# One plain block in place of two at the start of the last three channel mixers, with the next block's weights finished ahead

## The chip, the cores and the metric

The kernel runs on one core of one Trainium2 chip. The metric is the device time of one execution in microseconds (us), the median of the runs; less is better.

## The reference

A decoder trunk of two layers over 512 tokens of width 1024, all in float32. Each layer is channel mixer, token mixer, channel mixer; the token mixer of the first layer is latent attention, that of the second is sparse attention. So there are four channel mixers, numbered `idx` 0 to 3 here. Cut to what matters:

```python
D_MODEL, SEQ, DEPTH, FFN_HIDDEN = 1024, 512, 2, 2816

def swiglu(x, w_gate, w_up, w_down):
    return (jax.nn.silu(x @ w_gate) * (x @ w_up)) @ w_down

for i in range(DEPTH):
    h = h + 0.5 * swiglu(rmsnorm(h, ffn_norm_a[i]), ffn_a_w_gate[i], ffn_a_w_up[i], ffn_a_w_down[i])
    h = h + mixer_i(rmsnorm(h, mix_norm[i]))
    h = h + 0.5 * swiglu(rmsnorm(h, ffn_norm_b[i]), ffn_b_w_gate[i], ffn_b_w_up[i], ffn_b_w_down[i])
return rmsnorm(h, final_norm)
```

## The kernel before

The activations stand transposed: eight tiles `h[c]` of 128 features by 512 tokens. Every float32 operand of a matmul is split into a high part (a copy rounded by ScalarE) and a low part (the rest, subtracted by VectorE), and a product is three matmuls: high by high, high by low, low by high (`split`, L173; L177 and L178). So each weight costs a DMA, a ScalarE copy and a VectorE subtraction before TensorE can use it.

A channel mixer (`ffn`, from L416) goes through the 22 blocks of 128 hidden units, `f` = 0 to 21. A block computes gate and up for 128 hidden units and 512 tokens, then Silu(gate) x up in parts (`gate`, `act`, `parts`). It comes in two forms:

- **Plain** (`plain`, L404): gate, then up, each 8 chunks of input features times 2 halves of the tokens times 3 matmuls of 256 columns.
- **Seven products** (`product`, L371): gate and up together are a 2 by 2 problem (weights: gate and up, each with two halves of the input features; inputs: two halves of the features, each with two halves of the tokens). A scheme of the Strassen kind does it in 7 products of 4 chunks times 3 matmuls of 256 columns. It needs sums of weights (`wsums`, L328: products 1 and 2 take the gate's weights as they are, 7 and 4, 6 and 3, and 5 take sums) and sums of inputs (`combine`, L231: once per mixer, four calls with `p` = 0 to 3, each giving a quarter of what products 4 to 7 read).

`PLAIN = 3, 2, 2, 2` (L50) says how many blocks at the start of each mixer are plain. While they run, ScalarE and VectorE make the sums of inputs, and the norm's row (1/rms per token) is made: four small matmuls and more (`norm_col`), a transposition, and a round trip through DRAM on POOL's queue (`norm_row`, L293 and L295). The plain blocks don't need the row; their gate does (`plain_acts`, L428 to L430, L439).

The weights of the plain blocks of mixers 1 to 3 are split ahead of time. From block `READY` = 12 of the mixer before, each block loads one eighth (256 KB, `make_load`, L388, on SP's queue) and splits the one that it loaded a block earlier into two spare quarters of the input tiles; POOL's queue writes them to DRAM (`make`, L396). `made_slab` (L401) later reads high and low of a whole slab of 1 MB in one DMA. All other blocks load gate and up raw (`rg`, L333; `ru` or `wr`, L339; 512 KB each) and make sums and splits on the spot.

What sets the order: a scheduler lays down one fixed order for each engine and each DMA queue from the order of the program and estimates of when things are ready; every queue then works in that order. Buffers come from pools with tags: `fh` and `fl` (three each) hold the sums of inputs while they are made (`y`, `u`) and the split weights of products 7, 4, 6, 3; the tiles `w0` to `w2` hold plain slabs and the weights of products 1 and 2; `fr` (three) and `wr` (two) hold raw weights. In PSUM the tags are `mm` (2 banks), `S` (2), `T` (3), `o` (1). A block of seven products uses one bank of each of the first three: `x` (S), `q` (mm), `g` (T). The products go in the order 1, 7, 6, 2, 5, 4, 3, with ScalarE copying intermediate results out of the banks between them (L533, L535, L537, L540). From block 3 on, units of the down projection (`unit`, L169 to L171 on TensorE, L464, L458) are mixed into the blocks.

## Time and profile before

| | us |
|---|---|
| median of 3 runs | 1856.08 |
| lowest, highest run | 1854.83, 1859.17 |
| the profiled execution | 1855.04 |
| its span in the profile | 1853.3 |
| start of the plain blocks of mixers 1, 2, 3 in the span | 543.2, 877.7, 1507.2 |

The profile is one execution. A row of a timeline has the start in us from the span's beginning, the duration, the engine (PE is TensorE, PEld its weight loads, DVE is VectorE, ACT is ScalarE, POOL is GpSimd, SP the queue that issues most DMAs), the line of the kernel, the operation, the tile written and those read, and in brackets how long the engine sat idle before it and what ended that. A row of grouped instructions has the count, the busy time in us, the mean in ns, and the idle time before them. A row of windows has the stretch, its length, then busy time (and count) for PE, PEld, DVE, ACT and POOL, then the granted clock of TensorE, the busy share of the DMA engines, and GB/s. A row of waits has who waited for whom, the sum in us, how often, and the longest. A row of DMA issues has what is written and read, the queue, the count, the size of each, and the median time from issue to landing.

### The profile page before, as it was taken

To read this page: it belongs to the slowest core of one execution; us is meant where nothing else is said; L and a number is where in the kernel's file an instruction comes from. 1 tells how busy PE (TensorE), PEld (TensorE's weight loads), DVE (VectorE), ACT (ScalarE), POOL (GpSimd) and SP (SyncE) were. 2 spreads that over 40 slices of the span, in tenths; PEclk is the share of its full clock that TensorE was granted. 3 is DMA by queue.
4 is the path that set the end of the run, shared out by engine and by line. 5 is a ranking of instruction groups with operands and counts; after the bars stand their busy time and mean duration, and the time that the engine had idled before them with its cause. 6 is when DMAs were issued, how large, how long until landed. Compare 5 with 4: busy or idle time off the path is not lost.

```text
span 1853.3 us, 32953 instructions
## 1 busy us (share of the span) xinstructions
PE 1834.6 (99%) x12392; PEld 1674.9 (90%) x12392; DVE 1529.1 (83%) x2785; ACT 1090.8 (59%) x2033; POOL 275.9 (15%) x398
## 2 busy tenths in 40 slices
PE   8999999999999999999999999999999999999998
PEld 8999999888889999998999999988888889999997
DVE  7988886578779888876998888755988979888885
ACT  7555554579766555544655555426977856555554
POOL 0000000156510000000000000015665500000000
PEclk9999999999999999999999999999999999999999
DMA  7334433142352345433333443233222143333321
GB/s 259 118 120 154 154 124 105 56 110 72 95 176 99 105 143 166 160 115 122 110 115 130 161 160 99 91 106 108 75 86 74 47 163 121 108 107 103 103 90 57
DMA packets 88047, 216.31 MB, mean 117 GB/s; under 512 B 11176, under 2 KB 39232, under 8 KB 87888
## 3 DMA queue, kind: packets, MB, share of 16 engines
q1 hardware_dynamic: 80272, 195.01, 33.2%
q0 software_dynamic: 4512, 14.17, 2.0%
q10 hardware_dynamic: 3104, 5.03, 0.8%
q8 instruction: 97, 1.59, 0.4%
q14 instruction: 62, 0.51, 0.1%
HBM read 192.33 MB, written 14.76 MB: 112 GB/s over the span
## 4 chain that ended last, share of the span: by engine, by line
PE 87%; DVE 7%; ACT 2%; issue 1%; DMA 1%; POOL 1%; SPq 0%; DVEq 0%; ACTq 0%; POOLq 0%
PE pd L169 8%; PE pd L171 8%; PE pd L170 8%; PE px L376 5%; PE px L377 5%; PE px L378 5%; PE pg L376 4%; PE pg L378 4%; PE pg L377 4%; PE pq L376 4%; PE pq L377 4%; PE pq L378 4%; PE o L1295 2%; PE pt L1270 2%; PE po L169 2%; PE po L171 2%
## 5 line engine op out<-in xcount | busy, mean ns | idle before, releaser
L170 PE MATMUL pd<-al,wd 128*128 128x512 f32 x576 | 224.1, 389 | 0.0
L171 PE MATMUL pd<-ah,wd 128*128 128x512 f32 x576 | 224.0, 389 | 0.0
L169 PE MATMUL pd<-ah,wd 128*128 128x512 f32 x576 | 224.0, 389 | 0.0
L376 PE MATMUL px<-four,wh 128*128 128x256 f32 x632 | 175.3, 277 | 2.8 <-ACT uq L537 1.4
L178 DVE TENSOR_TENSOR w<-rg,w 128x1024 fp32r<-128x1024 f32 x79 | 96.3, 1222 | 96.4 <-ACT w L177 96.4
L376 PE MATMUL pq<-four,wh 128*128 128x256 f32 x632 | 174.5, 276 | 0.4 <-DVE tu L439 0.4
L378 PE MATMUL px<-four,wl 128*128 128x256 f32 x632 | 174.7, 276 | 0.0
L377 PE MATMUL px<-four,wh 128*128 128x256 f32 x632 | 174.5, 276 | 0.0
L377 PE MATMUL pq<-four,wh 128*128 128x256 f32 x632 | 174.5, 276 | 0.0
L378 PE MATMUL pq<-four,wl 128*128 128x256 f32 x632 | 174.5, 276 | 0.0
L458 DVE SCALAR_TENSOR_TENSOR h<-pd,h 128x512 f32<-128x512 f32 x216 | 147.0, 681 | 6.1 <-PE pd L171 6.1
L177 ACT ACTIVATE wd<-wdr 128x384 fp32r<-128x384 f32 x192 | 98.5, 515 | 67.9 <-PE pd L170 38.3
L171 PEld LDWEIGHTS pd<-ah,wd 128*128 128x128 f32 x576 | 108.2, 188 | 22.5
L169 PEld LDWEIGHTS pd<-ah,wd 128*128 128x128 f32 x576 | 108.1, 188 | 19.3
L170 PEld LDWEIGHTS pd<-al,wd 128*128 128x128 f32 x576 | 108.1, 188 | 19.4
L376 PEld LDWEIGHTS px<-four,wh 128*128 128x128 f32 x632 | 118.6, 188 | 4.1 <-ACT uq L537 2.1
L177 ACT ACTIVATE w<-rg 128x1024 fp32r<-128x1024 f32 x79 | 83.8, 1060 | 61.9 <-PE pg L378 56.6
L376 PEld LDWEIGHTS pq<-four,wh 128*128 128x128 f32 x632 | 118.6, 188 | 0.5 <-ACT w L177 0.5
L378 PEld LDWEIGHTS px<-four,wl 128*128 128x128 f32 x632 | 118.6, 188 | 0.4 <-DVE wl L178 0.2
L396 POOL DMA_DIRECT2D made<-x x48 | 26.0, 542 | 622.9 <-ACT pg L533 404.5
L377 PEld LDWEIGHTS px<-four,wh 128*128 128x128 f32 x632 | 118.6, 188 | 0.0
L378 PEld LDWEIGHTS pq<-four,wl 128*128 128x128 f32 x632 | 118.6, 188 | 0.0
(368 smaller groups left out, 6059.6 us busy)
## 6 DMA issues: line engine op xcount, KB each, us to landing
wr<-in_w_gu SPq DMA_DIRECT2D x81, 512.0 KB, 4.1
rg<-in_w_gu SPq DMA_DIRECT2D x79, 512.0 KB, 3.4
wdr<-in_w_down SPq DMA_DIRECT2D x192, 192.0 KB, 2.4
made<-x POOLq DMA_DIRECT2D x48, 256.0 KB, 2.8
w<-made SPq DMA_DIRECT2D x12, 1024.0 KB, 5.3
wm<-in_w_gu SPq DMA_DIRECT2D x24, 256.0 KB, 3.9
wdr<-in_w_down SPq DMA_DIRECT2D x24, 256.0 KB, 2.7
wr<-in_mla_w_o SPq DMA_DIRECT2D x8, 512.0 KB, 3.6
```

The source lines that it names most:

```text
L169: mm(out, wh, xh, start=first, stop=False)
L170: mm(out, wh, xl, start=False, stop=False)
L171: return mm(out, wl, xh, start=False, stop=last)
L177: nc.scalar.activation(hi, src, AF.Copy)
L178: (nc.gpsimd if pool else nc.vector).tensor_tensor(lo, src, f32v(hi), op=ALU.subtract)
L376: mm(out, wh[:, p], xh, start=first and p == 0, stop=False, skip_group_check=True)
L377: mm(out, wh[:, p], xl, start=False, stop=False, skip_group_check=True)
L378: mm(out, wl[:, p], xh, start=False, stop=last and p == KP - 1, skip_group_check=True)
L396: self.nc.gpsimd.dma_start(d[:, z, i % 2, :], f32v(t))
L458: nc.vector.scalar_tensor_tensor(self.h[c], p, 0.5, self.h[c], op0=ALU.mult, op1=ALU.add)
L1270: nc.tensor.transpose(pt[:, j * P : j * P + P], p_sb[:, j * P : j * P + P], self.ident)
L1295: mm(out, vs[g][:, j, br * P : (br + 1) * P], x, start=False, stop=last and t == 1 and j == 2 * z + 1, skip_group_check=True)
```

## The change

Mixers 1 to 3 start with one plain block and not two; block `f` = 1 becomes a block of seven products. All four `combine` calls follow the one plain block. The finished weights of that block, sums included, are made in the mixer before, as the plain slabs' were: `PLACES` says at which block `f` each piece is begun. For one plain block these are four eighths of plain slabs (blocks 9 to 11, each split a block later) and two halves of the sums (begun at blocks 12 and 16, four steps over four blocks each: load, then three with splits and 256-wide adds). What block 1 needs is read back as one slab of 1 MB (`g`: products 1 and 2, into a `w` tile), two pairs of 512 KB (`u`: 7 and 4; `h`: 6 and 3; into `fh` and `fl`) and one pair of 256 KB (`s`: 5). In that block alone the products are ordered 1, three quarters of 7, half of 2, the last quarter of 7, 6, the rest of 2, 5, 4, 3. `wsums` for `f` = 2 is now the one held behind the ScalarE copies of the block before it.

```diff
-PLAIN = 3, 2, 2, 2
+PLAIN = 3, 1, 1, 1
-READY = 12
+PLACES = {2: [...],
+          1: [(9, 0, 0, 0), (9, 0, 0, 1), (10, 0, 1, 0), (11, 0, 1, 1), (12, 1, 0, 0), (16, 1, 0, 1)]}
...
         nc, fp, w_gu = self.nc, self.fp, self.a["w_gu"]
+        if (idx, f, "g") in self.made:
+            return self.made_sums(idx, f)
...
-    def product(self, j, w, out, first, last):
+    def product(self, j, w, out, first, last, ps=range(KP)):
...
+    def make_sums(self, idx, f, x, tp):
...
+        def load():
+            for z in range(2):
+                got.append(self.make_load(self.a["w_gu"][idx, f, z].rearrange("p (e x c) -> p e x c", e=2, x=2)[:, :, x]))
...
+        def first():
+            self.make_split(got[0], 0, to("g"))
+            got.append(tp.tile([P, S], F32, tag="sq", bufs=1, name="sm")[:, :HS])
+            u = got[1]
+            nc.vector.tensor_tensor(got[2], u[:, :HS], u[:, HS:], op=ALU.add)
+            nc.vector.tensor_tensor(u[:, :HS], u[:, :HS], got[0][:, :HS], op=ALU.add)
+
+        def second():
+            self.make_split(got[1], 1, to("u"))
+            g = got[0]
+            nc.vector.tensor_tensor(g[:, :HS], g[:, :HS], got[2], op=ALU.add)
+            nc.vector.tensor_tensor(g[:, HS:], g[:, HS:], g[:, :HS], op=ALU.add)
+
+        def third():
+            self.make_split(got[0], 0, to("h"))
+            self.make_split(got[2], 1, self.made_tile(idx, f, "s").rearrange("p (z x c) -> p z x c", z=4, x=2)[:, :2, x])
...
+    def made_sums(self, idx, f):
...
+        use(1, 2, *self.made_slab(idx, f, "g"))
+        for name, i, j in (("u", 7, 4), ("h", 6, 3)):
+            hl = self.sum_tiles(1024)
+            for z in range(2):
+                nc.sync.dma_start(f32v(hl[z]), self.made[idx, f, name][:, z * 1024 : z * 1024 + 1024])
+            use(i, j, *hl)
+        hi = fp.tile([P, S], F32R, tag="sh", bufs=2, name="wh")
+        lo = fp.tile([P, S + 2 * PAD], F32R, tag="sl", bufs=2, name="wl")[:, 2 * PAD :]
+        for z, t in enumerate((hi, lo)):
+            nc.sync.dma_start(f32v(t), self.made[idx, f, "s"][:, z * S : z * S + S])
+        use(5, None, hi, lo)
+        return w
...
-            for p in (((0, 1), (2, 3)) if plain == 2 else ((0, 1), (2,), (3,)))[f]:
+            for p in {1: ((0, 1, 2, 3),), 2: ((0, 1), (2, 3)), 3: ((0, 1), (2,), (3,))}[plain][f]:
                 self.combine(p)
...
-            self.product(7, w, q, True, False)
+            self.product(7, w, q, True, False, range(KP - (f == 1)))
+            if f == 1:
+                self.product(2, w, g[:, :HS], False, False, range(2))
+                self.product(7, w, q, False, False, range(KP - 1, KP))
...
-            self.product(2, w, g[:, :HS], False, True)
+            self.product(2, w, g[:, :HS], False, True, range(2 * (f == 1), KP))
...
-            if idx + 1 < len(PLAIN):
-                i = f - READY
-                if 0 < i <= 4 * PLAIN[idx + 1]:
-                    self.make(idx + 1, i - 1)
-                if 0 <= i < 4 * PLAIN[idx + 1]:
-                    self.make_load(idx + 1, i)
+            for step in make.get(f, []):
+                step()
```

## The prediction

> **What bounds the kernel now.** I read the page first, then the windows around the second mixer's start, then TensorE's waits, then the timelines of each engine there.

> ```profile
> span 1853.3 us, 32953 instructions
> PE 1834.6 (99%) x12392; PEld 1674.9 (90%) x12392; DVE 1529.1 (83%) x2785; ACT 1090.8 (59%) x2033; POOL 275.9 (15%) x398
> L376 PE MATMUL px<-four,wh 128*128 128x256 f32 x632 | 175.3, 277 | 2.8 <-ACT uq L537 1.4
> ```
> ```profile
> 543.22:565.94 22.72, 22.72 (x202) 22.72 (x200) 21.07 (x34) 15.37 (x20) 2.30 (x3) 1.00 0.54 198
> 565.94:575.46 9.52, 9.52 (x87) 9.52 (x85) 9.37 (x13) 8.32 (x14) 0.00 (x0) 1.00 0.25 85
> 575.46:586.46 11.00, 9.96 (x86) 9.71 (x85) 11.00 (x19) 5.84 (x12) 0.00 (x0) 1.00 0.26 88
> ```

> TensorE is the bound nearly everywhere, so fewer matmuls should mean less time; the question is how much one costs. The first window holds the two plain blocks (192 matmuls and the 8 small ones of the norm), the second the first block of seven products (84 matmuls), the third the second such block. 9.52 / 84 = 0.113 us for a 256-column matmul. The 277 ns of its row is its stay in the pipeline, which overlaps its neighbours'. [...]

> VectorE (third busy column) is full through all three windows: the start of a mixer is where TensorE has company. Its waits there:

> ```profile
> PE px L376 <- ACT uq L537: 1.4, 2, 0.7
> PE px L376 <- ACT pg L533: 1.3, 2, 1.0
> 579.38 0.39 PE L376 MATMUL px<-four,wh 128*128 128x256 f32 x1 [1.04 <-ACT pg L533]
> 1545.92 0.39 PE L376 MATMUL px<-four,wh 128*128 128x256 f32 x1 [0.69 <-ACT uq L537]
> ```

> Each of the three mixers loses 1.04, 0.7 and 0.69 us in its second block of seven products, 2.4 us in all, with some 0.1 us for the restart (the matmul after a wait takes 0.39 us in place of 0.277).

> **Matmuls removed.** A plain block has 2 x 8 x 2 x 3 = 96 matmuls, a block of seven products 7 x 4 x 3 = 84. Each mixer swaps one: 12 x 0.113 = 1.36 us, three mixers 4.08 us. All of it is on TensorE's own path, where nothing covers it.

> **Combines, now due earlier.** Product 7 needs the sums of inputs at block f = 1, after one plain block and not two. In the second mixer the plain block would end at 543.22 + 96 x 0.113 + 0.95 (the norm's matmuls, what the first window leaves over 192 x 0.113) = 555.05. VectorE's rows of the four combines:

> ```profile
> 546.17 0.68 DVE L244 TENSOR_TENSOR u<-y 128x512 f32<-128x512 f32 x1
> 549.77 0.41 DVE L246 TENSOR_TENSOR u<-y,u 128x256 f32<-128x256 f32 x1
> 551.34 1.18 DVE L178 TENSOR_TENSOR four<-u,four 128x1024 fp32r<-128x1024 f32 x1
> 552.78 1.22 DVE L178 TENSOR_TENSOR four<-u,four 128x1024 fp32r<-128x1024 f32 x1
> ...
> 555.46 1.23 DVE L178 TENSOR_TENSOR four<-u,four 128x1024 fp32r<-128x1024 f32 x1
> ...
> 560.14 1.22 DVE L178 TENSOR_TENSOR four<-u,four 128x1024 fp32r<-128x1024 f32 x1
> ```

> The fourth ends at 561.4, behind four instructions on weights of the first block, which the change takes from there: two adds and two 1024-wide splits, 3.5 us by their starts (0.6, 0.6, 1.14, 1.14; each overlaps the next by 0.08). Without them it ends near 557.8, if ScalarE's halves keep up. Its user, the last quarter of product 7, stands behind product 1 (12 matmuls), three quarters of 7 (9) and half of 2 (6): 555.05 + 27 x 0.113 = 558.1. It just fits; I take 0. Without the new order product 7 would need it at 557.4, a wait of 0.4 us a mixer: that is what the order is worth.

> **Weights of block f = 1 from DRAM.** 7 and 4, then 6 and 3, come into tiles `fh`/`fl`, three buffers each, which the combines hold. I assume that buffers are handed out in program order: then the low half of 7 waits for the second combine's `u`, read last by L178 (552.78 + 1.22 = 554.0; the high half only for its `y`, free after L246 at 550.2), and the low half of 6 for the third's (about 556.7). No transfer of this kind is in the trace; the nearest are:

> ```profile
> rg<-in_w_gu SPq DMA_DIRECT2D x2, 512.0 KB, 3.1
> rg<-in_w_gu SPq DMA_DIRECT2D x1, 512.0 KB, 6.4
> 547.00:549.00 2.00, 2.00 (x21) 2.00 (x19) 2.00 (x5) 2.00 (x4) 0.00 (x0) 1.00 1.02 416
> 553.00:555.00 2.00, 2.00 (x20) 2.00 (x19) 2.00 (x4) 0.64 (x1) 0.00 (x0) 1.00 0.89 358
> 555.00:557.00 2.00, 2.00 (x20) 2.00 (x20) 2.00 (x4) 1.80 (x3) 0.10 (x1) 1.00 0.04 14
> ```

> 512 KB land in 3.1 us on a quiet queue (issues after 551) and 6.4 us behind others (issue at 543.98). At 554.0 the plain slabs and the slab for 1 and 2 should be in (the change has one slab less to bring before then than the kernel now), so I take 3.1: landing 557.15. Product 7 wants it at its third matmul, 555.05 + 14 x 0.113 = 556.6. Wait 0.5 us, with restart 0.65, times three: +1.95. Ends: 0 (the buffer is free sooner, or TensorE has other products ahead of it) and 3.95 a mixer (6.4 us). The low half of 6 lands by 559.9 and is wanted near 560.0: 0, at worst another 0.5. SP issues in order, so a transfer that waits for `fl` also holds back what stands behind it, the `rg`/`wr` of later blocks; they are due a block later, and I put that at 0.

> **VectorE's load at the start.** Rows for the sum:

> ```profile
> L178 DVE TENSOR_TENSOR w<-rg,w 128x1024 fp32r<-128x1024 f32 x79 | 96.3, 1222 | 96.4 <-ACT w L177 96.4
> L178 DVE TENSOR_TENSOR wl<-s,wh 128x512 fp32r<-128x512 f32 x79 | 53.9, 683 | 3.0 <-ACT wh L177 3.0
> L364 DVE TENSOR_TENSOR rg<-rg 128x512 f32<-128x512 f32 x79 | 54.5, 690 | 2.1
> L542 DVE TENSOR_TENSOR tu<-px,uq 128x256 f32<-128x256 f32 x79 | 32.9, 417 | 10.4 <-ACT pg L540 10.4
> ...
> 569.31 2.35 DVE L178 TENSOR_TENSOR w<-rg,w 128x1024 fp32r<-128x1024 f32 x2
> 574.04 1.22 DVE L178 TENSOR_TENSOR w<-rg,w 128x1024 fp32r<-128x1024 f32 x1
> ```

> One block's weights cost 3 x 1.22 + 0.68 + 4 x 0.69 = 7.1 us. Up to the third block f = 3 VectorE makes those of f = 2 and f = 3 before and after alike, since f = 1 got its weights from DRAM either way; the new block adds two adds of 0.42 us. So at f = 3 VectorE is 0.83 us later by work and TensorE 1.36 - 0.65 = 0.7 us earlier: up to 1.5 us more wait there. Against it: the weights of f = 2 no longer have to stand between the combines, and of the three splits of `rg` at 569.31 and 574.04 only one can be for f = 3, so VectorE worked 2.4 us ahead before that wait: its order has slack. Ends per mixer -0.9 (the wait goes) and +1.5; I take 0, the present wait staying.

> **The gate.** TensorE's `pu` bank of the plain block is wanted by product 7 of f = 2 at about 567; it used to be wanted a block later.

> ```profile
> 556.90 0.58 POOL L295 DMA_DIRECT2D row<-nrow  x1 [4.42 <-issue]
> DMA to landing us min/median/max: 3.4/3.7/4.2
> 563.09 1.28 DVE L428 TENSOR_TENSOR tg<-pg,row 128x512 f32<-128x512 f32 x2
> 564.34 1.28 ACT L429 ACT_TABLE_LOAD   x1
> L429 ACT ACTIVATE tg<-tg 128x512 f32<-128x512 f32 x88 | 55.3, 632 | 70.1 <-DVE tg L428 70.0
> 567.52 1.28 DVE L439 SCALAR_TENSOR_TENSOR tg<-pu,tg 128x512 f32<-128x512 f32 x2
> ```

> The row lands 3.7 us after its issue (the median of that line's six), 560.6; then product with the row 0.68, table 1.28, Silu 0.63, product 0.68, L439 0.68: 564.6, some 2 us ahead. I take 0; a wait of 1 us if VectorE puts splits between.

> **Making in the mixers before.** One more half block's worth than now: VectorE 4 x 0.68 + 2 x (3 x 0.68 + 4 x 0.42 + 0.42) = 11.0 us for each mixer against 8 x 0.68 = 5.4; POOL issues 24 transfers for 16 (0.54 us each, while POOL has nothing else). The blocks that carry it:

> ```profile
> L396 POOL DMA_DIRECT2D made<-x x48 | 26.0, 542 | 622.9 <-ACT pg L533 404.5
> 715.00:730.00 15.00, 15.00 (x108) 13.95 (x107) 13.32 (x22) 8.19 (x14) 1.09 (x2) 1.00 0.51 177
> 734.09 1.22 DVE L178 TENSOR_TENSOR w<-rg,w 128x1024 fp32r<-128x1024 f32 x1 [2.04 <-ACT w L177]
> ```

> VectorE has 1.7 us of 15 free there and TensorE doesn't wait; the heaviest new step adds 0.68 + 2 x 0.42 - 0.68 = 0.84. Hidden: 0. Without that cover, four such steps would cost 3.4 us a mixer.

> **Sum.** -4.08 + 1.95 = -2.1 us on the profiled execution's 1855.04 (1.74 outside its span): 1852.9. The median of the runs, 1856.08, lies 1.04 above it: 1854.0.

> **Rivals.** (1) The whole gain. The weights land in time, and VectorE, freed of splits between the combines, no longer makes f = 3 wait: -4.08, and up to 2.4 + 0.3 more: 1849.3 to 1852.0. For it: the 0.5 us is small, and a scheduler orders the instructions of each engine, which may put half of product 2 ahead. Against: VectorE is full for 30 us.
> (2) Slower: the low half of 7 lands late. If it stands behind the prefetched `rg`/`wr` of f = 2 and 3, it takes 6.4 us, the wait is 3.95, and 3 x 3.95 - 4.08 = +7.8: 1863.9. It costs all the gain from a wait of 1.36 us, and over 0.2% from 2.6 us (a landing of 5.1). Against: the quiet window 555 to 557. What a long wait can add:

> ```profile
> 5.93 0.58 PE L412 MATMUL pg<-x,w 128*128 128x256 f32 x1 [5.93 <-ACT w L150]
> 9.37 0.41 PE L413 MATMUL pg<-x,w 128*128 128x256 f32 x1
> 9.58 0.41 PE L414 MATMUL pg<-x,w 128*128 128x256 f32 x1
> ```

> After 5.9 us without work matmuls come 0.21 us apart; after 1.04 us (579.38) the granted clock stayed 1.00. [...]
> (3) VectorE is the bound of the start: f = 3 ends when VectorE does, 0.83 us later per mixer: +2.5, 1858.6. Its full windows speak for it.
> (4) The extra making shows in the blocks before: 3 x 3.4 - 2.1 = +8, 1862. TensorE's unbroken windows there speak against.
> That the change doesn't do what it says I exclude: the count of matmuls follows from PLAIN.

> **Numbers.** Forecast 0.40, rival 1 0.36, rival 2 0.13, rival 3 0.08, rival 4 0.03. A measurement of this kernel can tell some 0.2% (3.7 us) from no change; forecast and rival 3 lie within it: faster 0.36, same 0.48, slower 0.16. The range takes in rival 1 whole and rival 2 up to a wait of 3 us: 1849 to 1861; the likeliest case alone is 1852 to 1857.

> **What would show it.** 36 matmuls fewer; a block f = 1 of 9.5 us plus a wait of product 7 on a DMA of `wl`; the fourth combine done before that product's last quarter; the waits on `pg`/`uq` at f = 3 still there. I am wrong if product 7 doesn't wait, if those waits vanish or double, or if TensorE waits anywhere in the blocks that make weights.

## The result, and the profile after

| | median us | lowest, highest | runs |
|---|---|---|---|
| before | 1856.16 | 1854.83, 1859.17 | 4 |
| after | 1879.92 | 1877.99, 1881.23 | 4 |

The change makes the kernel slower by 1.25%: the ratio is 1.0125, with a 95% interval of 1.0107 to 1.0142. The forecast was 1854.0 with a range of 1849 to 1861; the result is far outside it.

The head of the page after, with busy time of TensorE and its count of matmuls:

```profile
span 1876.2 us, 33030 instructions
PE 1843.1 (98%) x12356; PEld 1679.4 (90%) x12356; DVE 1545.8 (82%) x2827; ACT 1098.3 (59%) x2057; POOL 295.7 (16%) x422
```

The 36 matmuls are gone (12392 to 12356), and yet TensorE is "busy" 8.5 us longer: matmuls that are stretched, as the windows below show. TensorE's waits over the whole span (sum in us, times, longest):

```profile
PE pq L379 <- ACT four L178: 9.9, 3, 3.8
...
PE pq L381 <- DMA wl<-made_u: 2.5, 2, 1.8
...
PE px L379 <- DMA wh<-made_h: 0.3, 1, 0.3
```

Product 7's bank `pq` waits three times, once a mixer, for the fourth tile of input sums (`four`). That is the heaviest new wait, and the prediction gave it 0. The wait for the low half of 7's finished weights, which it put at 1.95, is there too. What happens in mixer 1 is read from the queues in turn, first VectorE's timeline:

```profile
558.05 0.42 DVE L246 TENSOR_TENSOR u<-y,u 128x256 f32<-128x256 f32 x1
564.20 0.69 DVE L499 TENSOR_TENSOR tg<-pg,row 128x512 f32<-128x512 f32 x1 [5.72 <-DMA row<-nrow]
564.80 0.42 DVE L247 TENSOR_TENSOR u<-y,u 128x256 f32<-128x256 f32 x1
...
567.60 1.22 DVE L179 TENSOR_TENSOR four<-u,four 128x1024 fp32r<-128x1024 f32 x1
```

In VectorE's fixed order the plain block's gate (L499, the product with the norm's row) stands between the last two sums of the fourth combine (L246, L247). It waits 5.72 us for the row, and L247, which needs no row, waits behind it. ScalarE has the next piece, and then TensorE:

```profile
558.46 1.28 ACT L500 ACT_TABLE_LOAD   x1
564.92 0.63 ACT L500 ACTIVATE tg<-tg 128x512 f32<-128x512 f32 x1 [5.18 <-DVE tg L499]
565.46 1.04 ACT L178 ACTIVATE four<-u 128x1024 fp32r<-128x1024 f32 x1
```
```profile
560.64 0.39 PE L381 MATMUL pq<-four,wl 128*128 128x256 f32 x1 [0.70 <-DMA wl<-made_u]
...
566.55 0.58 PE L379 MATMUL pq<-four,wh 128*128 128x256 f32 x1 [3.75 <-ACT four L178]
```

The rounding of the fourth tile comes behind Silu (L500), and TensorE has nothing to do for 3.75 us. Why the row is late: its second transfer was issued at 558.46 (before: 556.90; the stage began 1.45 us later, which leaves 0.1), and it took 5.7 us, while the six of its kind before took 3.4 to 4.2. Three 512 KB loads of finished weights, issued at 555.48, 555.92 and 558.16, were under way beside it, one of which is shown (last column: median us from issue to landing):

```profile
558.46 0.58 POOL L296 DMA_DIRECT2D row<-nrow  x1 [4.64 <-issue]
```
```profile
wl<-made_u SPq DMA_DIRECT2D x1, 512.0 KB, 5.1
...
row<-nrow POOLq DMA_DIRECT2D x1, 256.0 KB, 5.7
```

And behind the wait comes a second loss. In windows of one us (the granted clock is the third number from the end):

```profile
565.00:566.00 1.00, 0.00 (x0) 0.00 (x0) 1.00 (x2) 1.00 (x2) 0.00 (x0) 1.00 0.00 0
566.00:567.00 1.00, 0.45 (x1) 0.29 (x1) 0.96 (x3) 1.00 (x2) 0.00 (x0) 0.67 0.00 0
567.00:568.00 1.00, 0.63 (x3) 0.50 (x3) 1.00 (x2) 1.00 (x2) 0.00 (x0) 0.50 0.00 0
...
572.00:573.00 1.00, 1.00 (x7) 1.00 (x6) 0.97 (x3) 0.00 (x0) 0.00 (x0) 0.50 0.00 0
573.00:574.00 1.00, 1.00 (x10) 1.00 (x9) 0.62 (x1) 0.00 (x0) 0.00 (x0) 0.92 0.52 147
```

TensorE runs at half clock from 566.3 to 573.2. The sum of (1 - clock) over one-us windows is 3.41 us here, 1.70 in mixer 2 and 3.41 in mixer 3, 8.5 us in all; before it was 0 at these places.

Where the time went follows from the first matmuls of each stage: from the start of the plain block to the first matmul of block 4 ("start"), and from there to the next mixer's plain block ("rest", where the making runs), each less the same stretch before. In mixer 0 the rest is all that comes ahead of mixer 1.

| us against before | mixer 0 | 1 start | 1 rest | 2 start | 2 rest | 3 start |
|---|---|---|---|---|---|---|
| after | +1.5 | +7.4 | +0.6 | +4.9 | +0.4 | +8.3 |

The starts cost 20.6 us: waits of 9.9 + 2.5 + 0.3, 8.5 of low clock, less 4.1 for the matmuls, make 17.1; the other 3.5 are waits under 1 us and restarts, which I did not tell apart.

### The profile page after: what moved, and what is told of

Its sections match the earlier page's. It is cut to its first block, busy times and chain, and to the rows that moved or that the text cites. A ratio compares the mean times of both kernels' runs of the same rounds, so it can differ in the third digit from the quotient of the medians.

```text
span 1876.2 us, 33030 instructions
## 1 busy us (share of the span) xinstructions
PE 1843.1 (98%) x12356; PEld 1679.4 (90%) x12356; DVE 1545.8 (82%) x2827; ACT 1098.3 (59%) x2057; POOL 295.7 (16%) x422
## 5 line engine op out<-in xcount | busy, mean ns | idle before, releaser
L379 PE MATMUL pq<-four,wh 128*128 128x256 f32 x656 | 182.8, 279 | 10.6 <-ACT four L178 9.9
L379 PE MATMUL px<-four,wh 128*128 128x256 f32 x656 | 184.3, 281 | 1.9 <-ACT pg L611 1.3
L381 PE MATMUL pq<-four,wl 128*128 128x256 f32 x656 | 182.3, 278 | 2.6 <-DMA wl<-made_u 2.5
L381 PE MATMUL px<-four,wl 128*128 128x256 f32 x656 | 183.4, 280 | 0.0
L380 PE MATMUL px<-four,wh 128*128 128x256 f32 x656 | 182.9, 279 | 0.0
L380 PE MATMUL pq<-four,wh 128*128 128x256 f32 x656 | 182.4, 278 | 0.1
L178 ACT ACTIVATE wd<-wdr 128x384 fp32r<-128x384 f32 x192 | 98.7, 515 | 71.4 <-PE pd L171 39.4
L379 PEld LDWEIGHTS pq<-four,wh 128*128 128x128 f32 x656 | 124.0, 189 | 11.6 <-ACT four L178 10.5
L379 PEld LDWEIGHTS px<-four,wh 128*128 128x128 f32 x656 | 124.9, 190 | 3.9 <-ACT pg L611 2.3
L381 PEld LDWEIGHTS pq<-four,wl 128*128 128x128 f32 x656 | 124.0, 189 | 3.2 <-DMA wl<-made_u 3.2
L381 PEld LDWEIGHTS px<-four,wl 128*128 128x128 f32 x656 | 125.3, 191 | 0.4 <-DVE wl L179 0.4
L380 PEld LDWEIGHTS px<-four,wh 128*128 128x128 f32 x656 | 124.9, 190 | 0.0
L380 PEld LDWEIGHTS pq<-four,wh 128*128 128x128 f32 x656 | 124.1, 189 | 0.6 <-DVE four L179 0.6
L178 ACT ACTIVATE w<-rg 128x1024 fp32r<-128x1024 f32 x79 | 83.6, 1060 | 59.6 <-PE pg L381 53.1
## 6 DMA issues: line engine op xcount, KB each, us to landing
wr<-in_w_gu SPq DMA_DIRECT2D x84, 512.0 KB, 4.2
rg<-in_w_gu SPq DMA_DIRECT2D x79, 512.0 KB, 3.5
wr<-in_mla_w_o SPq DMA_DIRECT2D x8, 512.0 KB, 3.5
```

The lines of the kernel that those rows point to most:

```text
L178: nc.scalar.activation(hi, src, AF.Copy)
L379: mm(out, wh[:, p], xh, start=first and p == 0, stop=False, skip_group_check=True)
L380: mm(out, wh[:, p], xl, start=False, stop=False, skip_group_check=True)
L381: mm(out, wl[:, p], xh, start=False, stop=last and p == KP - 1, skip_group_check=True)
```

## The experiments

The theory has parts, called so in the later expectations (those of runs 1 to 4 name their own): **G**, the gate waits for the row ahead of the fourth combine in VectorE's fixed order; **D**, the row and the finished weights' loads take longer beside one another (the row 5.7 us in the changed kernel, 3.4 to 4.2 before); **V**, VectorE has more to do under one plain block than fits there, whatever the order; **C**, the granted clock falls to 0.50 after such waits, for 6.83, 3.41 and 6.83 us in the changed kernel, which adds 8.5 us to the loss. The rivals: making is what costs; one plain block would do but for a single instruction's place. The same table for all runs but run 10 (in the last column the run's median and that of the kernel before, measured beside it):

| us against before | mixer 0 | 1 start | 1 rest | 2 start | 2 rest | 3 start | median, before |
|---|---|---|---|---|---|---|---|
| gate behind the combine | +3.7 | +3.1 | +0.4 | +0.8 | +1.2 | +2.9 | 1867.63, 1857.08 |
| and Silu behind copies | +2.7 | +2.3 | +0.9 | +1.4 | +0.5 | +2.4 | 1865.16, 1857.08 |
| two plain, finished | +2.5 | +6.2 | +2.0 | +1.5 | +1.0 | +4.4 | 1875.88, 1857.08 |
| busy in the wait | +3.0 | +9.6 | +0.5 | +4.9 | +0.4 | +4.7 | 1881.15, 1857.08 |
| made on the spot | +0.2 | +5.1 | +0.3 | +5.3 | +0.2 | +5.3 | 1872.80, 1856.31 |
| making, unread | +5.3 | 0.0 | +2.5 | 0.0 | +0.5 | 0.0 | 1862.27, 1856.31 |
| second combine on GpSimd | +2.5 | +5.1 | +0.6 | +5.2 | +0.7 | +8.9 | 1875.71, 1856.31 |
| loads and sums later | +2.1 | +10.2 | +0.7 | +6.7 | +2.4 | +9.4 | 1889.47, 1856.31 |
| on the spot, pinned | -0.2 | +5.8 | +0.1 | +5.1 | +0.5 | +5.6 | 1872.42, 1857.29 |
| the same, order undone | +3.1 | +4.3 | 0.0 | +5.2 | +0.7 | +6.6 | 1875.41, 1857.29 |
| third block later | +2.6 | +2.7 | +0.7 | +1.7 | +0.2 | +3.5 | 1866.97, 1856.99 |

Each row is one execution, taken against one execution of the kernel before, whose 1855.04 us lies 1 to 2 below the medians of the last column. How far executions of one order lie apart is seen in the two "on the spot, pinned" rows: their instructions stand in the same order on every engine and queue (see run 11), and yet mixer 0 differs by 3.3 us and two of the starts by 1.5 and 1.0. Differences of that size between two rows show nothing by themselves.

### 1 and 2: the gate, then Silu, out of the way

```diff
# 1
+            with self.tc.issue_after(self.combined.ins) if idx and f < plain else nullcontext():
                 nc.vector.tensor_tensor(t, g, row, op=ALU.mult)
# 2, on top of 1; plain_acts() is called behind copies[2]
+            with self.tc.issue_after(copies[2].ins) if idx and f < plain else nullcontext():
                 nc.scalar.activation(t, t, AF.Silu, scale=-1.0)
```

`combined` is the low half of the fourth combine's split. Expected of the first:

> The changed kernel with one edit: on VectorE the plain block's gate (its first product with the norm's row) is held behind the last instruction of the fourth combine, in mixers 1 to 3. Theory A (the gate waits for the row's DMA at the head of VectorE's queue, with the fourth combine behind it): product 7's waits on the fourth combine, 9.9 us in the changed kernel, vanish and the granted clock stays near 1.00; the gate's Silu still stands ahead of ScalarE's copies out of PSUM, which leaves a wait of 1 to 3 us per mixer: 1858 to 1870 us. Theory B (the finished weights land too late): no change, 1877 to 1882. Theory C (VectorE has too much to do at the start): the wait moves to another product, 1874 to 1882.

Measured: 1867.63 us, ratio 1.006 (1.0043 to 1.0077), so 13 of the 24 us are back. No wait for `four` is left, and the low clock costs 1.70 us in place of 8.5. Expected of the second:

> As the first, and the gate's Silu is held behind ScalarE's copies of products 1, 7 and 6 of block 1. Theory A: what is left per mixer are the waits on the finished weights, 0.5 to 2 us: 1852 to 1859 us. Theory B: 1877 to 1882. Theory C: above 1870.

Measured: 1865.16, ratio 1.0045 (1.003 to 1.006): better again, but above the 1859 expected. One order of two instructions was half the loss, which settles G; the rest has other causes. TensorE's waits in the second run, mixers 1 to 3:

```profile
PE pq L382 <- DMA wl<-made_u: 2.6, 2, 1.3
PE pg L380 <- ACT pg L614: 2.2, 1, 2.2
```

The 2.2 is ScalarE's copy of product 1 (L614) standing behind the rounding of the fourth tile, whose sums VectorE finishes only at 560.2. Behind that wait the granted clock fell to 0.50 again, which cost 1.7 us.

### 3: two plain blocks, with the finished weights

```diff
-PLAIN = 3, 1, 1, 1
+PLAIN = 3, 2, 2, 2
```

> The changed kernel with two plain blocks again in mixers 1 to 3 (36 matmuls more) and the finished weights for the first block of seven products, f = 2, made in the mixer before as in the change. Theory A: the combines are wanted 11 us later than in the changed kernel, so no wait on them; VectorE is freed of 7.1 us at the start: 1851 to 1858 us. Theory B: the finished weights land late here as well: a wait on made tiles of 1 us or more in each mixer, above 1860. Theory D (the extra making in the mixers before is what costs): above 1865.

Measured: 1875.88, ratio 1.0098 (1.0083 to 1.0113). A second plain block was to give the combines their time back, and it gave back only a part: 18.8 us over the kernel before in place of 23.8. The total is that of the extra making (above 1865), but 12.1 of the profile's 17.7 us lie in the starts. First VectorE in mixer 1, then the row's transfer there:

```profile
568.28 0.69 DVE L499 TENSOR_TENSOR tg<-pg,row 128x512 f32<-128x512 f32 x1 [8.73 <-DMA row<-nrow]
568.89 0.41 DVE L247 TENSOR_TENSOR u<-y,u 128x256 f32<-128x256 f32 x1
```
```profile
row<-nrow POOLq DMA_DIRECT2D x1, 256.0 KB, 8.8
```

The same knot, tighter: the plain slabs and the finished weights are loaded together, the row takes 8.8 us where it took 3.6 before, and the gate again stands ahead of L247. TensorE waits 3.1 us for the fourth tile and 7.2 for ScalarE's copy of product 1 in the three starts. So it isn't one plain block that makes the row late; it is what is loaded beside it.

### 4: matmuls into the wait

Eighteen matmuls into the half of bank `g` that product 3 uses are added ahead of product 7's last quarter; that half of the block's numbers is thereby changed.

```diff
+                with self.tc.issue_after(last.ins):
+                    for _ in range(18):
+                        last = nc.tensor.matmul(g[:, HS:], w[1][0][:, 0], self.xc["L", 0][0], ...)
```

> The changed kernel with 18 matmuls of 256 columns, whose result is written over later, put in front of product 7's last quarter in block 1 of mixers 1 to 3: TensorE works for 2 us of the wait. The waits stay. Theory A with the clock (after a wait of over 2 to 3 us TensorE runs at half clock for some 4 to 7 us): the granted clock stays 1.00 and the kernel is 8 to 13 us faster than the changed one: 1867 to 1872. If the clock costs nothing and the waits are all: 1880 to 1884.

Measured: 1881.15, ratio 1.0126 (1.0111 to 1.0142). The low clock cost 3.41 us in place of 8.5 (mixer 1 alone), but the pinned order kept TensorE from the parts of products 6 and 2 that it did in the wait before, and the sum is no better: it is the one expected if the clock cost nothing. That the clock fell in one mixer and not in three speaks for C; it gives no price.

### 5: one plain block, weights made on the spot

```diff
-          1: [(9, 0, 0, 0), (9, 0, 0, 1), (10, 0, 1, 0), (11, 0, 1, 1), (12, 1, 0, 0), (16, 1, 0, 1)]}
+          1: [(9, 0, 0, 0), (9, 0, 0, 1), (10, 0, 1, 0), (11, 0, 1, 1)]}
```

> One plain block, but the weights of the first block of seven are made on the spot as in all others, so no 3.5 MB of finished weights are loaded beside the norm's row. Theory D (the finished weights' loads crowd the two row transfers, which took 4.7 and 5.7 us after the change where they took 3.4 and 3.7 before): the row lands near 561, the gate hardly waits, and the three starts lose 3 us or less each: 1860 to 1866. Theory G (VectorE's fixed order alone): the gate still stands ahead of the fourth combine's split, so TensorE still waits 3 us or more for the fourth tile and the clock still falls: 1870 or more. Theory V (VectorE has too much to do under one plain block): about 7 us more of splits and sums stand in VectorE's queue at each start than with finished weights: 1880 or more, with waits for splits of the weights.

Measured: 1872.80, ratio 1.0094 (1.0076 to 1.0112): faster than the whole change, though all the splits of that block are back on VectorE. The total lies in G's range (1870 or more), but not for G's reason: no matmul waits for the fourth tile. The row's transfers in mixer 1, without loads of finished weights beside them:

```profile
row<-nrow POOLq DMA_DIRECT2D x1, 256.0 KB, 3.3
nrow<-row POOLq DMA_DIRECT2D x1, 2.0 KB, 1.7
```

3.3 and 1.7 us in place of 5.7 and 4.7 (before the change 3.6 and 4.4): that is D, in two numbers. The gate stands ahead of the fourth split here too and doesn't wait. What TensorE waits for now is VectorE and what feeds it:

```profile
PE pq L381 <- DVE wl L179: 3.7, 3, 1.2
PE pq L379 <- ACT wh L178: 2.8, 3, 0.9
PE px L381 <- DVE w L179: 2.1, 3, 0.7
PE pg L379 <- ACT pg L611: 1.4, 3, 0.5
```

3.3 us a mixer in four waits, and then 1.7 of low clock in each. My total for D (1860 to 1866) missed: with the row cured, V stood there in its place, at less than the 1880 that I gave it.

### 6: making alone

Before's two plain blocks and weights made on the spot, while the sums are made and written in the mixer before and read by nobody.

```diff
-PLAIN = 3, 1, 1, 1
+PLAIN = 3, 2, 2, 2
...
-        if (idx, f, "g") in self.made:
-            return self.made_sums(idx, f)
```

> Two plain blocks, every block of seven made on the spot in its own order, as before the change; the finished sums are made in the mixer before and written to DRAM, and nobody reads them. The prediction's step (making is hidden): 1856, no difference. The rival from the block starts (a making step moves a unit's split ahead of the copy of product 1 in ScalarE's fixed order, and that split waits for its load): 1.5 to 3 us more, nearly all in mixer 0 at two or three blocks: 1858 to 1860.

Measured: 1862.27, ratio 1.0032 (1.002 to 1.0044), above both expectations. The starts cost nothing (the table), the making does. Of mixer 0's 5.3 us, 3.0 come at block 3, ahead of any making: a wait of 2.31 us for VectorE's `tu` and the low clock behind it. That is not the edit's doing. Up to there every engine works in the order of the kernel before, whose profile has the same wait with 0.36 us, and runs 9 and 11, alike in order, have it with 0.29 and 2.43 (a load of the inputs, `xt`, took 3.4 us in the one and 7.1 in the other). The other 2.3, and 2.5 and 0.5 in the next mixers, come where pieces are made. How, is seen on ScalarE at block 4 of mixer 1:

```profile
600.68 0.63 ACT L178 ACTIVATE x<-wm 128x512 fp32r<-128x512 f32 x1 [2.30 <-DMA wm<-in_w_gu]
601.22 0.37 ACT L609 ACTIVATE pg<-px 128x256 f32<-128x256 f32 x1
```

The split of a piece (`wm`) stands ahead of the copy of product 1 and waits 2.30 us for its load, and TensorE waits 0.87 us for the copy. In the changed kernel, at block 14 of mixer 0, it is the split of a unit's weights:

```profile
212.35 0.52 ACT L178 ACTIVATE wd<-wdr 128x384 fp32r<-128x384 f32 x1 [3.89 <-DMA wdr<-in_w_down]
212.78 0.37 ACT L611 ACTIVATE pg<-px 128x256 f32<-128x256 f32 x1
```

The same two before the change:

```profile
210.67 0.37 ACT L533 ACTIVATE pg<-px 128x256 f32<-128x256 f32 x1 [1.11 <-PE px L378]
211.78 0.53 ACT L177 ACTIVATE wd<-wdr 128x384 fp32r<-128x384 f32 x1 [0.74 <-DMA wdr<-in_w_down]
```

With the making's steps mixed in, the order puts a unit's split ahead of the copy of product 1; the split waits 3.89 us for its load, and TensorE, which wants the copy, waits 0.83. Neither VectorE's nor ScalarE's total is the matter. The size is surer than one profile makes it: the seven profiles of kernels that make the sums at the change's places (the changed kernel and runs 1, 2, 4, 7, 8 and 12, with one order in mixer 0) lose 1.2 to 3.5 us at blocks 8 to 14 of mixer 0, and the three that leave the sums out (5, 9 and 11) lose nothing there.

### 7, 8 and 12: taking more away

Run 7 stands on run 2: the second combine's sums and split go to GpSimd, and the fourth tile's rounding behind the copy of product 1.

```diff
-                self.combine(p)
+                four = self.combine(p, nc.gpsimd if idx and p == 1 else None, bool(idx) and p == 3)
...
             copies = [nc.scalar.activation(g[:, :HS], x, AF.Copy)]
+            if f == plain and idx:
+                with self.after(copies, 0):
+                    four()
```

> The version with gate and Silu moved behind, and further: the second combine's three sums and its split on GpSimd, and the fourth tile's rounding on ScalarE behind the copy of product 1. Theory V (VectorE's 2.75 us per combine is the bound of the start): the fourth tile is ready 1.5 to 2.7 us earlier and the 2.2 us wait for product 1's copy is gone, and with it the drop of the clock (1.7 us): 1859 to 1862. Rival D (the next late thing is the low half of product 7's finished weights, which lands 5 us after its issue): TensorE waits 1 to 2 us for it in every start, 1862 to 1865. Rival: GpSimd's own sums are slow or delay the row: over 1866.

Measured: 1875.71, ratio 1.0107 (1.0091 to 1.0123), 11 us worse than run 2, each against its kernel before. First GpSimd, then VectorE:

```profile
556.58 2.46 POOL L179 TENSOR_TENSOR four<-u,four 128x1024 fp32r<-128x1024 f32 x1
```
```profile
556.69 2.63 DVE L247 TENSOR_TENSOR u<-y,u 128x256 f32<-128x256 f32 x1
```

A sum that takes VectorE 0.42 us took 2.63 and ended 0.3 us after GpSimd's split (in mixers 2 and 3 a sum beside that split took 3.07 and 3.14): nothing was won on VectorE. And the `u` of the second combine, which the low half of 7's weights takes over, came free at 559.1 and not at 556.7, so that TensorE waited 4.1 us for that load. Run 8 goes further: loads of the second and third block behind the finished weights', their splits and sums behind later copies, the gate behind the second block's first split.

```diff
+        with self.tc.issue_after(self.made_load.ins) if idx and f in (PLAIN[idx] + 1, PLAIN[idx] + 2) else nullcontext():
             self.gate_load = nc.sync.dma_start(rg, w_gu[idx, f, 0])
```

> As the run before it, with everything of the second and third block of seven held back: their loads behind the loads of the finished weights, their sums and splits behind the copy of product 1, and the plain block's gate behind the second block's first split. Theories V and D together (the start is bound by VectorE's queue and by what the transfers share): hardly any wait is left at the starts, the three starts take 4 us less than in the two-plain-block kernel less what the second block then waits: 1855 to 1860. Rival: what is held back comes late in its turn, and TensorE waits 1 us or more for the second block's weights in each mixer: 1861 or more.

Measured: 1889.47, ratio 1.0174 (1.0156 to 1.0192). It missed widely, for the same reason and one more: SP now issued the high half of 6 ahead of the low half of 7, and TensorE waited 4.6, 4.0 and 3.9 us for the latter. But its row took 3.7 us in mixer 1 and the step before it 1.7, with less loaded beside them, which is D a second time. Run 12 mends both: no GpSimd, the finished weights in the order of use, only the third block's load behind them.

> The finished weights kept, gate and Silu moved behind as in the second experiment, and further: the third block's first load (0.5 MB) behind the finished weights' loads, its first split and the second block's sums behind later copies, and the fourth tile's rounding on ScalarE behind the copy of product 1. GpSimd does none of the combine. Theories V and D together: the row's two transfers take about 1 us less, the fourth tile is ready 1.9 us earlier, the 2.2 us wait for the copy of product 1 is gone, 1 us or less is left waiting for the low half of product 7's weights, and the clock falls nowhere: each start costs 0 to 1 us, and what is left is the making in mixer 0 (1.5 to 2.7 us): 1857 to 1861. Rival: the low half of product 7's weights is late by 2 us or more whatever stands around it, and the clock falls with it: 1863 or more.

Measured: 1866.97, ratio 1.0051 (1.0037 to 1.0064), no better than run 2. The wait for the copy is gone, and in its place, in the same start (TensorE, mixer 1):

```profile
560.86 0.39 PE L390 MATMUL pq<-four,wl 128*128 128x256 f32 x1 [1.49 <-DMA wl<-made_u]
...
566.12 0.39 PE L390 MATMUL px<-four,wl 128*128 128x256 f32 x1 [1.59 <-DMA wl<-made_h]
```

In mixer 3 the wait for `wl` was 1.96 us, and the granted clock fell to 0.50 behind it, which cost 1.7 us. That is the bottom of it: in mixer 1 both low halves go into buffers that the combines hold until 556.6 and 559.3, and land 4.2 and 6.8 us later. The rival of the expectation holds. VectorE's fourth split still ended at 562.4.

### 9 and 11: on the spot, pinned, and the order of products

Run 9 puts the pins of run 2 on run 5 and holds the first splits of the second and third block behind copies; run 11 was to undo the own order of products in it (the "first run" of its text is run 9).

```diff
# 9
-            w = self.wsums(idx, f, copies if idx and f == plain + 1 else None)
+            w = self.wsums(idx, f, copies if idx and f in (plain + 1, plain + 2) else None)
# 11
-            if f == 1:
+            if False:
                 self.product(2, w, g[:, :HS], False, False, range(2))
```

> One plain block, the first block of seven's weights made on the spot, the plain block's gate behind the fourth combine's split and its Silu behind the block's third copy, and the second and third block's first splits held back behind later copies. Theory V (VectorE's queue bounds the start, and what stands ahead of the fourth combine and of product 7's split there is what costs): two splits of 1.22 us and a gate of 0.68 us go from ahead of them, so of the 3.3 us of waits per start in the run with the gate ahead about 1 to 2 are left, none long enough for the clock to fall: the three starts cost 0 to 2 us each in place of 5.3: 1856 to 1862. Rival: the fixed order fills the free places with other sums, and the waits and the drop of the clock stay: 1867 or more.

> As the first run of this call, but the first block of seven takes its products in the order of all other blocks: product 7 whole, no part of product 2 ahead of its last quarter. Theory: TensorE then needs the fourth tile 0.68 us sooner in each of the three starts: 1 to 2 us more in all. Rival: product 7 waits for its own weights or the copy by then, and the order is worth nothing: within 0.5 us.

Measured: 1872.42, ratio 1.0086 (1.0071 to 1.01), and 1875.41, ratio 1.0096 (1.008 to 1.0112). Run 9 is run 5 over again: the scheduler filled the freed places with other sums of the same block, and the waits in mixer 1 are the same:

```profile
PE pq L382 <- DVE wl L179: 1.3, 1, 1.3
PE pq L380 <- ACT wh L178: 1.1, 1, 1.1
PE px L382 <- DVE w L179: 0.7, 1, 0.7
PE pg L380 <- ACT pg L614: 0.5, 1, 0.5
```

Its rival holds: the work is there, not only its order (V). Run 11 tests nothing: the scheduler lays down the same order on every engine and queue for both, with the whole of product 2 ahead of product 7. They are two sets of executions of one order; the 3 us between their medians are scatter (the runs reach from 1870.82 to 1877.52 and from 1872.45 to 1877.46), and in the two profiles they lie in mixer 0. What the own order is worth stays open.

### 10: waits by hand

The kernel before, with idle copies of product 1 ahead of the true one.

```diff
+            for _ in range(DELAY.get((idx, f), (0, 0))[0]):
+                nc.scalar.activation(uq[:, :HS], x, AF.Copy)
             copies = [nc.scalar.activation(g[:, :HS], x, AF.Copy)]
```

> The kernel before the change, with idle copies put on ScalarE ahead of product 1's copy in six blocks of seven, so that TensorE waits there by a set amount (copies at 0.28 us each, less the 1.36 us of the product in between): about 1.4, 2.3, 3.1 and 4.2 us, once two of 1.4 within 5 us, once two of 2.3. No work is left out. Theory C (the clock halves after a wait of somewhat over 2 us, or after shorter ones close together, and stays so for 3.41 us, which costs 1.7): no loss after 1.4, 1.7 after 2.3 and 3.1, 3.4 after 4.2; total about 1856 plus 19 of waits plus 8 to 10 of low clock, 1883 to 1887. Rival (the low clock in the changed kernel came from something else at the starts): no window below full clock, 1875.

Measured in one run: 1867.07. No window at these blocks is below full clock, but neither are the waits what I set:

```profile
PE px L377 <- ACT pg L536: 3.5, 4, 1.4
```

The scheduler moved units of the down projection into the gaps, and the longest wait was 1.4 us. It shows that one wait of 1.4 us did not lower the clock, and nothing on longer ones. Mixer 0 became 1.1 us longer here, with a wait of 1.5 us at `tu`, though every engine's order there is that of the kernel before.

## Why the prediction was wrong

- **Matmuls removed: right.** 36 fewer.
- **The gate: the step that failed.** "The row lands 3.7 us after its issue … 560.6 … I take 0." It was issued 1.6 us later than before (1.45 of it the stage's own) and took 5.7 us: landing 564.2. I priced the row from a trace in which little was loaded beside it, and named that quiet window as the case against contention, while the change fills just that window with finished weights. And I asked only who waits for the gate, not what stands behind it in VectorE's queue while it waits. Putting it behind the fourth combine gave 13 us back.
- **Combines: failed too, hidden by the first.** "It just fits; I take 0": the fourth combine was to end 14.6 us after the plain block's start, 0.3 ahead of its user. Where no gate blocks it (runs 1, 2 and 12) it ends 16.6 us after, 562.4 - 545.8 in run 12: 2.0 late. Its last sum ends 14.3 us after in all three, and behind it stand ScalarE's rounding (1.06) and VectorE's subtraction (1.2), one after the other. The "near 557.8" left no room for these two: in the kernel before, the last sum itself ended only at 557.96. An add for a later block (0.69) had also taken the place of one of those that went.
- **Weights from DRAM: the issue right, the size off.** The low half of 7 was issued at 555.48; without the 1.45 us by which the stage began later that is the predicted 554.0. But it took 5.1 (mixers 2 and 3: 4.5 and 4.2) and not 3.1 us. The waits were 0.70 and 1.83, and none in mixer 3, where TensorE waited 0.91 for the copy of product 1 and the half landed meanwhile: 2.5 in all against 1.95. Rival 2 is what is left once the rest is cleared away (run 12), at 1.4 to 2.0 us a mixer for 7, not 3.95, and again 0.9 to 1.6 for 6.
- **The clock.** The forecast has no loss of this kind, since I saw no long wait. The low clock cost 3.41, 1.70 and 3.41 us in the three mixers behind waits of 3.75, 2.32 and 3.80, and 1.70 behind 2.21 and 1.96 in runs 2 and 12.
- **Making: "Hidden: 0" failed.** It cost some 2.5 us in the changed kernel's profile (1.5, 0.6, 0.4), not by VectorE's load, but by splits that wait for a load and stand ahead of a copy on ScalarE. Rival 4, which asked for this, has a slip in its sum: 3.4 us in each mixer on top of the forecast would be 1864, not 1862.
- **Rival 3** (VectorE bounds the start) was right in kind, as runs 5 and 9 show, and too small: it has to be asked of the fourth combine, not of block 3.

What stays open: what the own order of products is worth, and whether a smaller set of finished weights, or more buffers for the sums, so that the low halves could be loaded sooner, would pay. None of these was tested.

## What to carry to other kernels

Before moving work earlier, write down for each engine what stands in its queue in the new window, and ask of every instruction that may wait (here a product with a row from DRAM) what would stand behind it. Price a transfer by the traffic that will be beside it after the change, not by the trace before: the same 256 KB of the row in mixer 1 took 3.6 us before, 5.7 in the changed kernel, 8.8 in run 3 and 3.3 in run 5. And one profile is no measure of a stage: where every engine's order was the same, mixer 0 still took up to 3 us more or less from one execution to the next, so a stage's difference of that size needs several profiles.

## What the runs showed of the hardware

The clock fell after shorter waits than I thought (over 2 to 3 us, in run 4's text), and the length of one wait does not decide it. It fell after 1.96 us without a matmul (run 12, mixer 3), 2.21 (run 2) and 3.75 (the changed kernel, mixer 1); after 1.74 (run 3, mixer 2) and even after 2.43 (run 11, mixer 0) it didn't. In runs 9 and 11 six starts had the same waits of some 0.5, 1.1 and 1.3 us within 5 us, and it fell in four of them. Mixer 1 and mixer 3 of run 9, each in the two us behind those waits:

```profile
565.00:567.00 2.00, 2.00 (x12) 2.00 (x11) 2.00 (x3) 0.32 (x1) 0.00 (x0) 0.50 0.35 70
1539.00:1541.00 2.00, 1.70 (x14) 1.49 (x14) 2.00 (x4) 1.80 (x3) 0.00 (x0) 1.00 0.62 238
```

```profile
41.46:44.87 3.41, 2.25 (x20) 2.05 (x19) 2.69 (x5) 3.38 (x4) 0.00 (x0) 1.00 0.59 175
44.87:48.28 3.41, 2.14 (x18) 2.17 (x19) 3.41 (x7) 2.39 (x6) 0.00 (x0) 1.00 0.54 179
```
```profile
41.45:44.86 3.41, 1.24 (x11) 1.04 (x10) 2.69 (x5) 2.41 (x3) 0.00 (x0) 1.00 0.58 204
44.86:48.27 3.41, 3.27 (x15) 3.31 (x16) 3.41 (x7) 2.31 (x5) 0.00 (x0) 0.50 0.22 67
```

VectorE's sums took longer beside GpSimd's two-input split in run 7. In mixer 1 a sum of 0.42 us took 2.63; the split, of 2.46, had begun 0.1 us before it. In mixers 2 and 3 the sum began first, by 0.37 and 0.18 us, and took 3.07 (0.42 elsewhere) and 3.14 (0.69 elsewhere) beside splits of 2.41. The three sums ended 0.28, 0.29 and 0.55 us after the split.
